# The attention output product by seven block products per pair of tiles, with its operands built beside late input tiles

## The chip, the core and the metric

One core of a Trainium2 chip runs the kernel as one program. The metric is the device time in microseconds, as the median over several executions. TensorE (PE in the profile) does the matmuls; VectorE (DVE), ScalarE (ACT) and GpSimd (POOL) prepare operands and take results out of PSUM; DMA queues, nearly all issued by SyncE (SP), move the data.

## The reference

One layer of a streaming encoder for a prompt of 1024 frames and a sample of 32 frames, model width 1024, all in float32. What matters here is the first part of the layer:

```python
h = rms_norm(x, g_mix)
z = h @ w_in
q, k, v, ch, cb, cc, ga, gb = jnp.split(z, SPLITS, axis=-1)
...
a = attn_core(q, k, v) @ w_attn_out
...
bo = (cb * conv) @ w_conv_out
x = x + (jax.nn.sigmoid(ga) * a + jax.nn.sigmoid(gb) * bo) @ w_mix_out
```

Behind it come a cross attention into 256 memory tokens, a squared-ReLU MLP of width 4096 and a final norm.

## The kernel before

All 1056 frames are kept transposed (features on the partitions) and cut into three chunks, CH, of 384, 384 and 288 columns: chunks 0, 1 and 2. A weight tile is 128 outputs by 1024 inputs (0.5 MB). Each float32 operand is split into a high and a low part (`split`: ScalarE casts the high part, line 120; VectorE subtracts, line 121), and a product takes three matmuls per 128 inputs: high by high, high by low, low by high (`gemm`, lines 176 to 178). A tile by one chunk is thus 24 matmuls.

The program writes a list of items (`item`, `run`) with the weights that each needs. `next_w` keeps two weights split ahead and one more in flight (`wr`); a STOP in the list of weights ends this running ahead, and `resume` takes it up again. The frame's scheduler then orders the instructions of each engine; each engine and SP's DMA queue works strictly in its order.

In the input projection the tiles from the second `b` on go in pairs (`x_pair`): two output tiles by chunks 0 and 1 form a two by two block product, and it is done by seven products of half the inputs (12 matmuls of 384 columns) instead of eight. For this the four operand kinds T2, N1, N3 and N4 are built once from the inputs (`x_kind`: line 801 to 805 differences, line 812 the high casts, lines 814 on VectorE and 816 on GpSimd the low parts, into tiles `tk` and the slots `X1`), and for each pair the weight sums s31 and s24 by four GpSimd additions (lines 834 to 837, `pair_issue`). `product` issues the matmuls (lines 852 to 854). Chunk 2 of each pair is done by plain products beside (`x_c2`, tiles `pa`). `x_start` opens the pairs with the products that need raw weights only; `x_steps` hangs weight splits and fetches on points of the pair before.

The last three pairs (LATE = 3) leave chunk 2 out. Their six tiles' chunk-2 products come as single items behind all pairs, with the raw weights loaded and split a second time; beside them the attention outputs, which were stored to `ao_d`, are loaded back into `ct` and split into the `Y` slots (`load_split`, line 1001), four per tile. Then `do_attn_out` multiplies them by `w_attn_out`: for tiles f = 0 to 3 all chunks, then f = 4 to 7 chunk by chunk (weights split again each time), each result times the gate `sg` into `m1_d`. Beside the later of these products the operands of the next stage (conv output, `bcp` from `bc_d`) are loaded and split.

GpSimd also prepares sums of `w_down` for the MLP in 32 pieces (`sum_load`, `sum_add`, `sum_step`, lines 726, 733, 734), spread over attention, pairs and late tiles.

In the trace, names such as `wh`, `wl` (weight high and low), `wr`, `wr2` (raw weights of a pair), `lt` and `ct` (temporaries), `acc` and `pa` (PSUM) are the tags of these tiles.

## Time and profile before

| | us |
|---|---|
| timed runs | 1795.58, 1793.97, 1791.87 |
| median | 1793.97 |
| profiled execution, its time | 1797.28 |
| its span | 1795.5 |
| attention, with parts of the projection | to about 414 |
| operand kinds and start of the pairs | about 414 to 458 |
| pairs | about 458 to 687 |
| late chunk-2 tiles | about 687 to 706 |
| attention output product | about 706 to 788 |
| conv output and mix | about 788 to 873 |

The lower rows are stretches of the profiled execution's time axis, told by the lines of TensorE's matmuls. A group's "idle before" is the time in which its engine stood still ahead of it, with what ended it; idle time of an engine matters where TensorE waits for that engine. In tables of windows the granted clock is that of TensorE, 1.00 being full speed.

### The profile page before, as it was taken

The page shows a single profiled execution, that of the slowest core. Times are in us where ns is not written, and L with a number is a line of the kernel's source. Part 1 is how long each engine was busy: PE and PEld are TensorE (multiplying, and loading weights), DVE is VectorE, ACT ScalarE, POOL GpSimd, SP SyncE. Part 2 cuts the span into 40 slices and gives each one's busy share as a digit, 9 for nine tenths or more (in the row PEclk, how much of TensorE's full clock was granted, in tenths as well). Part 3 has the DMA queues.
Part 4 walks back from the last instruction along what each step waited for, and adds up shares of the span by engine and source line. Part 5 has one row for each costly group of instructions (what it writes and reads, how often), then busy time and mean ns, then how long its engine had stood idle before and what let it go on. Part 6 is the DMA issues. An engine that isn't in the chain of part 4 may idle for free.

```text
span 1795.5 us, 30126 instructions
## 1 busy us (share of the span) xinstructions
PE 1750.8 (98%) x11030; PEld 1723.8 (96%) x11030; DVE 1190.2 (66%) x2081; ACT 816.0 (45%) x1573; POOL 738.6 (41%) x777
## 2 busy tenths in 40 slices
...
GB/s 180 144 66 141 104 151 99 148 90 152 120 99 90 167 97 265 219 246 317 252 227 208 246 213 240 248 168 151 142 122 137 162 304 207 163 134 200 195 248 102
DMA packets 177828, 312.50 MB, mean 174 GB/s; under 512 B 18032, under 2 KB 137616, under 8 KB 177552
## 3 DMA queue, kind: packets, MB, share of 16 engines
...
q14 instruction: 61, 0.50, 0.1%
...
## 4 chain that ended last, share of the span: by engine, by line
PE 80%; DMA 7%; DVE 5%; ACT 3%; issue 2%; POOL 2%; SPq 1%; POOLq 0%; DVEq 0%; ACTq 0%
PE acc L176 10%; PE acc L177 10%; PE acc L178 10%; PE acc L852 6%; PE acc L854 6%; PE acc L853 6%; PE acc L1648 5%; PE acc L1649 5%; PE acc L1647 5%; PE pa L177 2%; PE pa L176 2%; PE pa L178 2%; DVE wl L121 2%; PE pt L577 2%; DMA ct<-in_x 1%
## 5 line engine op out<-in xcount | busy, mean ns | idle before, releaser
L120 ACT CAST wh<-wr 128x1024 fp32r<-128x1024 f32 (+1 forms) x223 | 233.2, 1046 | 320.7 <-PE acc L1648 81.0
L121 DVE TENSOR_TENSOR wl<-wr,wh 128x1024 fp32r<-128x1024 f32 (+1 forms) x223 | 307.6, 1379 | 103.1 <-ACT wh L120 102.4
L253 POOL TENSOR_TENSOR xacc<-xacc,ct 128x384 f32<-128x384 f32 (+1 forms) x62 | 77.8, 1257 | 321.9 <-ACT ct L251 319.3
L176 PE MATMUL acc<-X,wh 128*128 128x384 f32 (+1 forms) x624 | 204.7, 328 | 1.1 <-ACT wh L120 1.1
L176 PE MATMUL acc<-Y,wh 128*128 128x384 f32 (+1 forms) x624 | 203.1, 326 | 2.3 <-DVE ct L1140 1.2
L177 PE MATMUL acc<-Y,wh 128*128 128x384 f32 (+1 forms) x624 | 203.0, 326 | 0.9 <-DVE Y L121 0.8
L177 PE MATMUL acc<-X,wh 128*128 128x384 f32 (+1 forms) x624 | 202.3, 324 | 1.0 <-DVE X L257 1.0
L178 PE MATMUL acc<-Y,wl 128*128 128x384 f32 (+1 forms) x624 | 202.8, 325 | 0.4 <-DVE wl L121 0.4
L178 PE MATMUL acc<-X,wl 128*128 128x384 f32 (+1 forms) x624 | 203.0, 325 | 0.0
L569 POOL TENSOR_SCALAR S<-S,rec 128x256 f32<-128x256 f32 (+1 forms) x132 | 124.1, 953 | 49.5 <-DVE rec L567 49.1
L176 PEld LDWEIGHTS acc<-Y,wh 128*128 128x128 f32 x624 | 117.8, 189 | 3.3 <-ACT Y L120 1.7
L177 PEld LDWEIGHTS acc<-X,wh 128*128 128x128 f32 x624 | 118.0, 189 | 2.7 <-DVE X L257 1.8
L176 PEld LDWEIGHTS acc<-X,wh 128*128 128x128 f32 x624 | 117.9, 189 | 2.6 <-ACT wh L120 1.3
L177 PEld LDWEIGHTS acc<-Y,wh 128*128 128x128 f32 x624 | 118.0, 189 | 1.8 <-DVE Y L121 1.8
L178 PEld LDWEIGHTS acc<-Y,wl 128*128 128x128 f32 x624 | 118.1, 189 | 0.8 <-DVE wl L121 0.8
L178 PEld LDWEIGHTS acc<-X,wl 128*128 128x128 f32 x624 | 117.9, 189 | 1.0 <-DVE wl L121 0.2
L1647 PE MATMUL acc<-Y,wh 128*128 128x384 f32 (+1 forms) x352 | 113.7, 323 | 0.7 <-DVE lt L1403 0.7
L1648 PE MATMUL acc<-Y,wh 128*128 128x384 f32 (+1 forms) x352 | 113.9, 324 | 0.1
L1649 PE MATMUL acc<-Y,wl 128*128 128x384 f32 (+1 forms) x352 | 113.6, 323 | 0.0
L120 ACT CAST wh<-s 128x1024 fp32r<-128x1024 f32 x50 | 52.2, 1050 | 90.6 <-PE acc L853 53.8
L121 DVE TENSOR_TENSOR Y<-ct,Y 128x384 fp32r<-128x384 f32 (+1 forms) x128 | 70.7, 582 | 29.5 <-ACT Y L120 29.5
L120 ACT CAST Y<-ct 128x384 fp32r<-128x384 f32 (+1 forms) x128 | 59.5, 486 | 60.2 <-DMA ct<-bc_d 14.6
...
## 6 DMA issues: line engine op xcount, KB each, us to landing
wr<-in_w_in SPq DMA_DIRECT2D x55, 512.0 KB, 3.3
wr<-in_w_up SPq DMA_DIRECT2D x48, 512.0 KB, 4.0
wr<-in_w_down SPq DMA_DIRECT2D x32, 512.0 KB, 3.8
wr<-wsum_d SPq DMA_DIRECT2D x32, 512.0 KB, 3.6
wl<-wl_d SPq DMA_DIRECT2D x28, 512.0 KB, 4.6
wr<-in_w_conv_out SPq DMA_DIRECT2D x24, 512.0 KB, 4.6
wr<-in_w_mix SPq DMA_DIRECT2D x24, 512.0 KB, 4.4
xacc<-in_w_down POOLq DMA_DIRECT2D x20, 512.0 KB, 3.7
```

Of the source, the lines that this page charges most:

```text
L120: act.copy(hi, src)
L121: dve.tensor_sub(lo, src, hi.bitcast(F32))
L176: pe.matmul(out, wh[:, a], hi, start=(k == 0), stop=False)
L177: pe.matmul(out, wh[:, a], lo, start=False, stop=False)
L178: pe.matmul(out, wl[:, a], hi, start=False, stop=(k == len(acts) - 1))
L569: pool_e.tensor_scalar_mul(stl[:, h, :nk], stl[:, h, :nk], rec[:, h : h + 1])
L852: pe.matmul(acc, wh[:, a], hi, start=(start and k == 0), stop=False, skip_group_check=True)
L853: pe.matmul(acc, wh[:, a], lo, start=False, stop=False, skip_group_check=True)
L854: pe.matmul(acc, wl[:, a], hi, start=False, stop=(k == 3), skip_group_check=True)
L1647: pe.matmul(a, wh[:, s], hi, start=(start and k == 0), stop=False, skip_group_check=True)
L1648: pe.matmul(a, wh[:, s], lo, start=False, stop=False, skip_group_check=True)
L1649: pe.matmul(a, wl[:, s], hi, start=False, stop=(stop and k == len(acts) - 1), skip_group_check=True)
```

## The change

Chunks 0 and 1 of the attention output product become four more pairs (`("o", f)` in XP, indices from NX = the old count on), of seven block products each; chunk 2 stays plain, eight products with their own split of the weights. The operand kinds for these pairs come from `ao_d` (`a_kind`, which also splits the plain operands that the pairs use, into the `X` slots instead of a pool of their own). They are built beside the late chunk-2 tiles, which are four pairs' now (LATE = 4, eight tiles). For these eight tiles the low weights are stored once when the pair splits them (`again`, `kept`, `wl_d`), and read back, so that VectorE does not subtract again. `a_start` opens the new pairs as `x_start` does the old ones. The pieces of the weight sums move: two more in the attention stage, one in nearly every pair, none beside the late tiles. The operands of the mix chunk that were split beside the attention product come later (`loads(1)` in `do_mix`).

```diff
-        for k in ((5, 8, 11, 14), (2, 5, 8, 11, 14), (2, 5, 8, 11, 14), (2, 5))[kv]:
+        for k in ((5, 8, 11, 14), (2, 5, 8, 11, 14), (2, 5, 8, 11, 14), (2, 5, 8, 11))[kv]:
...
         split(hi, lo, raws[key][src])
         wset[key, which] = (hi, lo)
+        at = again.get((key, which))
+        if at:
+            kept[at] = dram.tile([P, 1024], F32, name=nm("wl_d"))
+            sp.dma_start(kept[at], lo.bitcast(F32))
...
-    LATE = 3
+    LATE = 4
+    NX = len(XP)
+    XP += [(("o", f), ("o", f + 1)) for f in (0, 2, 4, 6)]
...
+    again.update({(("x", i), half + 1): tile_key(XP[i][half]) for i in range(NX - LATE, NX) for half in range(2)})
...
+        elif i in (NX - 1, len(XP) - 1):
+            todo = {w: resume for w in ("W1", "W4", "W3")}
...
-            if what == "W3" and (i % 3 or i == len(XP) - 1):
+            if what == "W3" and 0 < i != NX and i != NX + 1:
                 sum_load(True)
+            if i >= NX and what in ("B11", "W1"):
+                loads(1)
...
+    def a_kind(k):
+
+        b12, b22, b11, b21 = lt(), lt(), tmp(384), tmp(384)
+        for t, c, f in ((b12, 1, k), (b22, 1, k + 4), (b11, 0, k), (b21, 0, k + 4)):
+            sp.dma_start(t, ao_d[c][:, f])
+        ...
+        keep(0, k, b11)
+        keep(0, k + 4, b21)
+        keep(1, k + 4, b22)
+        n3, n1, t2, n4 = b22, b12, b11, b21
+        dve.tensor_sub(n3, b12, b22)
+        dve.tensor_sub(n1, b11, b12)
+        dve.tensor_sub(t2, b11, n3)
+        pool_e.tensor_tensor(n4, b21, t2, op=ALU.subtract)
+        for kind, x in (("T2", t2), ("N1", n1), ("N3", n3), ("N4", n4)):
+            ...
+            act.copy(hi, x)
+            if kind in ("T2", "N1"):
+                dve.tensor_sub(lo, x, hi.bitcast(F32))
+            else:
+                pool_e.tensor_tensor(lo, x, hi.bitcast(F32), op=ALU.subtract)
...
+    def a_start():
+        x_issue(NX, 4)
+        A = x_p1(NX)
+        A2 = x_p1(NX + 1)
+        x_p2(NX, A)
+        x_issue(NX, 3)
+        x_p2(NX + 1, A2)
+
+    steps = [lambda k=k: a_kind(k) for k in range(4)]
+    steps.append(lambda: [x_fetch(NX), x_issue(NX, 1), x_fetch(NX + 1)])
+    steps.append(lambda: [x_issue(NX, 2), x_issue(NX + 1, 1)])
+    last = [t for pair in XP[NX - LATE : NX] for t in pair]
+    steps[4:4] = [lambda: None] * (len(last) - 6)
+    for t, step in zip(last, steps):
+        item(do_in(t, [(2, step)], (2,)), tile_key(t))
+    worder.append(STOP)
+    item(lambda: todo.extend((aop, ao_d, 2, k) for k in range(NF)))
+    item(a_start)
+    for i in range(NX, len(XP)):
+        item(lambda i=i: x_pair(i, x_steps(i), {NX: 2, NX + 1: 1}.get(i, 0)))
     item(lambda: todo.extend((bcp, bc_d, 0, k) for k in range(NF)))
+    for f in range(NF):
+        item(do_attn_out(f, lambda f=f: [sum_done(), loads(1)]), ("w_attn_out", f))
...
@@ (do_mix)
+            if c == 0:
+                loads(1)
```

The order of the instructions moves at three places. In each row stand the line, the operation, output and inputs with their buffer numbers, the shape, and what the instruction waits for. Lines from 850 on are numbered four higher after the change, and higher still further down.

TensorE at the start of the first pairs, before: the end of N3's product for pair 0 (`tk_988` and `tk_989` with `wh_1015`), the T2 product of pair 1 (`wh_1026` and `wl_1027`, the split s24 of that pair), then N4's product (`X1_952`) and that of the plain chunk 1 (`X1_54`), both of pair 0:

```order
L852 MATMUL acc_1028_5668<-tk_988_5409,wh_1015_5565 128x384 [waits Activation_49]
L853 MATMUL acc_1028_5668<-tk_989_5410,wh_1015_5565 128x384 [waits Pool_49]
L854 MATMUL acc_1028_5668<-tk_988_5409,wl_1016_5566 128x384
L852 MATMUL acc_1044_5766<-tk_946_5282,wh_1026_5664 128x384 [waits Activation_49]
L853 MATMUL acc_1044_5766<-tk_947_5283,wh_1026_5664 128x384
L854 MATMUL acc_1044_5766<-tk_946_5282,wl_1027_5665 128x384 [waits DVE_49]
...
L852 MATMUL acc_1028_5668<-X1_952_5294,wh2_1002_5487 128x384 [waits DVE_49]
...
L852 MATMUL acc_1029_5669<-X1_54_356,wh_1008_5501 128x384 [waits DVE_49]
```

The same place after:

```order
L856 MATMUL acc_1030_5682<-tk_990_5423,wh_1017_5579 128x384 [waits Activation_49]
L857 MATMUL acc_1030_5682<-tk_991_5424,wh_1017_5579 128x384 [waits Pool_49]
L858 MATMUL acc_1030_5682<-tk_990_5423,wl_1018_5580 128x384
L856 MATMUL acc_1030_5682<-X1_954_5308,wh2_1004_5501 128x384 [waits DVE_49]
...
L857 MATMUL acc_1030_5682<-X1_993_5428,wh2_1004_5501 128x384 [waits Pool_49]
...
L856 MATMUL acc_1031_5683<-X1_54_356,wh_1010_5515 128x384 [waits DVE_49]
...
L856 MATMUL acc_1046_5780<-tk_948_5296,wh_1028_5678 128x384 [waits Activation_49]
L857 MATMUL acc_1046_5780<-tk_949_5297,wh_1028_5678 128x384
L858 MATMUL acc_1046_5780<-tk_948_5296,wl_1029_5679 128x384 [waits DVE_49]
```

The two products of pair 0 with `X1_954` and `X1_54`, 24 matmuls, now stand ahead of the T2 product of pair 1 (`wh_1028`, `wl_1029`) instead of behind it.

GpSimd at the same place, before: the last N4 low (`X1_991`), the sums s31 and s24 of pair 1, and the last N3 low (`tk_989`):

```order
L816 TENSOR_TENSOR tk_977_5380<-xk_969_5358,tk_976_5379 128x384 [waits Activation_49]
L816 TENSOR_TENSOR X1_991_5414<-xk_983_5390,X1_990_5413 128x384 [waits PE_49,Activation_49]
L834 TENSOR_TENSOR s31_1024_5658<-wr2_999_5455 128x512 [waits DMAHW7_49,DVE_49]
L837 TENSOR_TENSOR s31_1024_5658<-wr_998_5454,wr2_999_5455 128x512
L816 TENSOR_TENSOR tk_989_5410<-xk_981_5388,tk_988_5409 128x384 [waits DMAHW1_49,Activation_49]
L835 TENSOR_TENSOR s24_1025_5659<-wr_998_5454,s31_1024_5658 128x512 [waits Pool_49]
L836 TENSOR_TENSOR s24_1025_5659<-wr_998_5454,s24_1025_5659 128x512 [waits Pool_49]
```

And after:

```order
L816 TENSOR_TENSOR tk_991_5424<-xk_983_5402,tk_990_5423 128x384 [waits DMAHW1_49,DVE_49,Activation_49]
L834 TENSOR_TENSOR s31_1026_5672<-wr2_1001_5469 128x512 [waits DMAHW7_49,DVE_49]
L837 TENSOR_TENSOR s31_1026_5672<-wr_1000_5468,wr2_1001_5469 128x512
L816 TENSOR_TENSOR X1_993_5428<-xk_985_5404,X1_992_5427 128x384 [waits PE_49,Activation_49]
L835 TENSOR_TENSOR s24_1027_5673<-wr_1000_5468,s31_1026_5672 128x512 [waits Pool_49]
L836 TENSOR_TENSOR s24_1027_5673<-wr_1000_5468,s24_1027_5673 128x512 [waits Pool_49]
```

The last N4 low (`X1_993`) has moved behind the two s31 additions, and the last N3 low (`tk_991`) ahead of them; s24 stands last in both.

VectorE beside the late chunk-2 tiles, before: gate emits (`Gb2`), splits of attention outputs (`Y1`) and weight lows (`wl`):

```order
L662 TENSOR_TENSOR Gb2_1430_8247<-acc_1429_8222,R_141_767 128x288 [waits PE_49]
L121 TENSOR_TENSOR Y1_1400_8129<-ct_1398_8126,Y1_1399_8128 128x384 [waits DMAHW6_49,Activation_49]
L121 TENSOR_TENSOR wl_1446_8284<-wr_1444_8281,wh_1445_8283 128x1024 [waits DMAHW7_49,DVE_49,Activation_49]
L662 TENSOR_TENSOR Gb2_1448_8312<-acc_1447_8287,R_141_767 128x288 [waits PE_49]
L121 TENSOR_TENSOR Y1_1403_8135<-ct_1401_8132,Y1_1402_8134 128x384 [waits DMAHW0_49,Activation_49]
L121 TENSOR_TENSOR Y1_1406_8141<-ct_1404_8138,Y1_1405_8140 128x384 [waits DMAHW1_49,Activation_49]
L121 TENSOR_TENSOR Y1_1415_8188<-ct_1413_8185,Y1_1414_8187 128x384 [waits DMAHW2_49,Activation_49]
L121 TENSOR_TENSOR wl_1464_8349<-wr_1462_8346,wh_1463_8348 128x1024 [waits DMAHW3_49,DVE_49,Activation_49]
L121 TENSOR_TENSOR Y1_1418_8194<-ct_1416_8191,Y1_1417_8193 128x384 [waits DMAHW4_49,Activation_49]
```

After, the third kind of the four (`lt_1414`, `lt_1415`, `ct_1416`) with its differences (lines 1041 to 1043), its T2 and N1 lows (line 1053), and the weight lows of the first two new pairs (`wl_1478`, `wl_1482`):

```order
L121 TENSOR_TENSOR X1_1423_8142<-lt_1415_8126,X1_1422_8141 128x384 [waits DMAHW5_49,Activation_49]
L662 TENSOR_TENSOR Gb2_1466_8332<-acc_1465_8307,R_141_767 128x288 [waits PE_49]
L1041 TENSOR_TENSOR lt_1415_8126<-lt_1414_8125,lt_1415_8126 128x384 [waits DMAHW1_49,DVE_49,Pool_49]
L1042 TENSOR_TENSOR lt_1414_8125<-ct_1416_8127,lt_1414_8125 128x384 [waits DVE_49]
L1043 TENSOR_TENSOR ct_1416_8127<-ct_1416_8127,lt_1415_8126 128x384 [waits DVE_49]
L121 TENSOR_TENSOR wl_1478_8380<-wr_1471_8343,wh_1477_8379 128x1024 [waits DMAHW7_49,DMAHW2_49,Activation_49]
L662 TENSOR_TENSOR Gb2_1474_8372<-acc_1473_8347,R_141_767 128x288 [waits PE_49]
L1053 TENSOR_TENSOR tk_1425_8150<-ct_1416_8127,tk_1424_8149 128x384 [waits Activation_49]
L121 TENSOR_TENSOR wl_1482_8390<-s24_1480_8384,wh_1481_8389 128x1024 [waits DMAHW6_49,Activation_49]
L1053 TENSOR_TENSOR tk_1427_8154<-lt_1414_8125,tk_1426_8153 128x384 [waits Activation_49]
```

The differences and the lows of the kinds stand between the emits where the `Y` splits stood.

GpSimd beside the late tiles, before, has only the sums of `w_down`:

```order
L726 DMA xacc_1461_8339<-in_w_down 128x1024 [waits DMASW2_49]
L733 TENSOR_TENSOR ws_1443_8274<-ws_1443_8274 128x256 [waits DMASW1_49]
L733 TENSOR_TENSOR ws_1443_8274<-ws_1443_8274 128x256 [waits Pool_49] x3
L734 DMA wsum_d_97<-ws_1443_8274 128x1024 [waits Pool_49]
L726 DMA ws_1467_8380<-in_w_down 128x1024 [waits DMASW4_49]
```

After, it has the ends of the kinds (n4 on line 1044, lows of N4 and N3 on line 1055) and the weight sums of the second new pair (`s31_1491`, `s24_1492`):

```order
L1055 TENSOR_TENSOR tk_1429_8158<-lt_1415_8126,tk_1428_8157 128x384 [waits Activation_49]
L1044 TENSOR_TENSOR ct_1440_8202<-ct_1440_8202,ct_1439_8201 128x384 [waits DMAHW3_49,DVE_49]
L834 TENSOR_TENSOR s31_1491_8462<-wr2_1472_8344 128x512 [waits DMAHW7_49,DVE_49]
L837 TENSOR_TENSOR s31_1491_8462<-wr_1471_8343,wr2_1472_8344 128x512 [waits DMAHW7_49]
L1055 TENSOR_TENSOR X1_1454_8236<-ct_1440_8202,X1_1453_8235 128x384 [waits PE_49,Activation_49]
L1055 TENSOR_TENSOR tk_1452_8232<-lt_1438_8200,tk_1451_8231 128x384 [waits Activation_49]
L835 TENSOR_TENSOR s24_1492_8463<-wr_1471_8343,s31_1491_8462 128x512 [waits Pool_49]
L836 TENSOR_TENSOR s24_1492_8463<-wr_1471_8343,s24_1492_8463 128x512 [waits Pool_49]
```

The second new pair's s24 is behind the last kind's lows.

TensorE behind the late tiles, before, goes over to the attention output product with the `Y` operands:

```order
L177 MATMUL acc_1447_8287<-X2_105_573,wh_1409_8153 128x288
L178 MATMUL acc_1447_8287<-X2_104_572,wl_1410_8154 128x288
L176 MATMUL acc_1465_8352<-Y0_1360_7992,wh_1427_8218 128x384 [waits DVE_49,Activation_49]
L177 MATMUL acc_1465_8352<-Y0_1361_7993,wh_1427_8218 128x384
L178 MATMUL acc_1465_8352<-Y0_1360_7992,wl_1428_8219 128x384 [waits DVE_49]
```

After: raw-weight products (`X0` operands), T2, N3 and N4 of the first new pair, and then the T2 product of the second (`wh_1493`, `wl_1494`, the split of `s24_1492`):

```order
L858 MATMUL acc_1483_8393<-X0_1372_7985,wl_1470_8340 128x384 [waits DVE_49]
...
L856 MATMUL acc_1498_8478<-tk_1378_8001,wh_1481_8389 128x384 [waits DVE_49,Activation_49]
L857 MATMUL acc_1498_8478<-tk_1379_8002,wh_1481_8389 128x384
L856 MATMUL acc_1483_8393<-X0_1374_7989,wh_1469_8339 128x384 [waits Activation_49]
...
L856 MATMUL acc_1498_8478<-tk_1382_8009,wh_1488_8438 128x384 [waits DVE_49]
L857 MATMUL acc_1498_8478<-tk_1383_8010,wh_1488_8438 128x384 [waits Pool_49]
...
L856 MATMUL acc_1498_8478<-X1_1384_8013,wh2_1475_8375 128x384 [waits DVE_49]
...
L856 MATMUL acc_1520_8585<-tk_1378_8001,wh_1493_8468 128x384 [waits Activation_49]
L858 MATMUL acc_1520_8585<-tk_1378_8001,wl_1494_8469 128x384 [waits DVE_49]
```

The first product that needs s24 of the second new pair is now that last group, 108 matmuls behind the last late tile.

98 lines of the change are left out of this document (43 added, 55 removed).

## The prediction

> **What bounds the kernel now.** First the head of the page and its shares of the chain:
>
> ```profile
> span 1795.5 us, 30126 instructions
> PE 1750.8 (98%) x11030; PEld 1723.8 (96%) x11030; DVE 1190.2 (66%) x2081; ACT 816.0 (45%) x1573; POOL 738.6 (41%) x777
> PE 80%; DMA 7%; DVE 5%; ACT 3%; issue 2%; POOL 2%; SPq 1%; POOLq 0%; DVEq 0%; ACTq 0%
> ```
>
> TensorE is busy for 98% of the span, so a matmul taken out is worth its step unless something makes TensorE wait instead. The step is read from the timeline of TensorE:
>
> ```profile
> 669.94 0.33 PE L854 MATMUL acc<-X,wl 128*128 128x384 f32 x1
> ...
> 675.31 0.33 PE L852 MATMUL acc<-X,wh 128*128 128x384 f32 x1
> 443.21 0.29 PE L178 MATMUL pa<-X,wl 128*128 128x288 f32 x1
> ...
> 444.00 0.29 PE L178 MATMUL pa<-X,wl 128*128 128x288 f32 x1
> ```
>
> From 669.94 to 675.31 lie 31 steps: 0.1732 us per matmul of 384 columns. From 443.21 to 444.00 lie six: 0.132 us for 288 columns. A product of 24 matmuls of 288 columns thus takes 3.17 us.
>
> Next the windows around the stages that the change touches. The columns are window and length, busy time and count of PE, PEld, DVE, ACT and POOL, granted clock, DMA share, GB/s:
>
> ```profile
> 450.00:460.00 10.00, 7.25 (x32) 6.61 (x31) 4.56 (x5) 2.52 (x3) 5.88 (x6) 0.83 0.26 87
> 455.00:690.00 235.00, 234.11 (x1439) 233.79 (x1439) 169.45 (x207) 77.34 (x102) 144.90 (x139) 0.99 0.35 118
> 690.00:705.00 15.00, 15.00 (x115) 15.00 (x115) 13.90 (x19) 9.46 (x19) 6.00 (x8) 1.00 0.88 293
> 705.00:710.00 5.00, 5.00 (x32) 5.00 (x32) 4.52 (x7) 3.05 (x6) 4.36 (x5) 1.00 1.02 388
> 710.00:725.00 15.00, 12.96 (x54) 11.35 (x53) 8.97 (x16) 5.68 (x13) 4.81 (x7) 0.77 0.86 296
> 780.00:785.00 5.00, 5.00 (x40) 5.00 (x39) 3.29 (x5) 2.29 (x4) 0.00 (x0) 1.00 0.96 299
> ```
>
> The pairs (455 to 690) lose almost nothing. Two places do: 450 to 460 and 710 to 725. What TensorE waits for there:
>
> ```profile
> 450.99 0.34 PE L854 MATMUL acc<-tk,wl 128*128 128x384 f32 x1
> 453.44 0.45 PE L852 MATMUL acc<-tk,wh 128*128 128x384 f32 x1 [2.11 <-ACT wh L120]
> 454.70 0.69 PE L854 MATMUL acc<-tk,wl 128*128 128x384 f32 x1 [0.64 <-DVE wl L121]
> 457.74 0.45 PE L854 MATMUL acc<-tk,wl 128*128 128x384 f32 x1
> 715.70 0.40 PE L176 MATMUL acc<-Y,wh 128*128 128x288 f32 x1 [0.86 <-ACT Y L120]
> 718.14 0.61 PE L177 MATMUL acc<-Y,wh 128*128 128x288 f32 x1 [0.77 <-DVE Y L121]
> 719.44 0.45 PE L178 MATMUL acc<-Y,wl 128*128 128x288 f32 x1
> ```
>
> At 453.44 it is the first product of the second pair (T2, with the weight sum s24 of that pair) that has come up before its weights are split. At 715.70 the attention outputs read back (ct from ao_d) land too late for their splits Y, while the DMA engines are full. After each stop the matmuls go on at a longer step for some us (granted clock 0.83 and 0.77 in the two windows).
>
> **The change, part by part.** The sum is made against the profiled execution's own 1797.3 us; the median of the runs is 1794.0, that is 3.3 lower, and I take 3.3 off at the end.
>
> *Fewer matmuls.* Chunks 0 and 1 took 16 products of 24; now four pairs of seven block products of 12. 384 − 336 = 48 matmuls, 48 × 0.1732 = **−8.3 us**. The chunk-2 products (eight of 24 for the output, eight of the four a-pairs' tiles) are the same number as before.
>
> *The old entrance goes.* In 710 to 725 stand 54 matmuls. Nine of them (715.70 to 719.44) have 288 columns: 45 × 0.1732 + 9 × 0.132 = 9.0 us of work in 15. So 6.0 us were lost to the Y splits, and those splits no longer stand there: **−6.0 us**. What is late in their place comes below.
>
> The two starts below are costed from rows of the first start, where VectorE and GpSimd build the same four operands (T2, N1, N3, N4) and the weight sums s31 and s24 (min, median and max in ns behind an xN:; a timeline row has its start and length):
>
> ```profile
> L801 DVE TENSOR_TENSOR xk<-xk,xk x4: 548/559/1000, 418.9 to 436.9; 128x384 f32<-128x384 f32 x4
> L814 DVE TENSOR_TENSOR tk<-xk,tk x8: 551/1368/1642, 423.4 to 446.0; 128x384 fp32r<-128x384 f32 x8
> L816 POOL TENSOR_TENSOR tk<-xk,tk x4: 1001/1324/1957, 424.3 to 448.7; 128x384 fp32r<-128x384 f32 x4
> L834 POOL TENSOR_TENSOR s<-wr x3: 1276/1598/1605, 425.6 to 456.3; 128x512 f32<-128x512 f32 x3
> L121 DVE TENSOR_TENSOR wl<-s,wh x4: 1208/1212/1226, 440.7 to 455.0; 128x1024 fp32r<-128x1024 f32 x4
> L733 POOL TENSOR_TENSOR ws<-ws x4: 752/941/1605, 694.1 to 697.6; 128x256 f32<-128x256 f32 x4
> L120 ACT CAST wh<-wr 128x1024 fp32r<-128x1024 f32 (+1 forms) x223 | 233.2, 1046 | 320.7 <-PE acc L1648 81.0
> 447.98 0.44 DVE L662 TENSOR_TENSOR ct<-pa,R 128x288 f32<-128x288 f32 x1
> 423.29 1.08 POOL L816 TENSOR_TENSOR X<-xk,X 128x384 fp32r<-128x384 f32 x1 [14.93 <-ACT X L812]
> 434.03 1.59 POOL L836 TENSOR_TENSOR s<-wr,s 128x512 f32<-128x512 f32 x1
> 443.87 1.75 POOL L816 TENSOR_TENSOR X<-xk,X 128x384 fp32r<-128x384 f32 x1 [1.04 <-ACT X L812]
> 447.14 1.61 POOL L837 TENSOR_TENSOR s<-wr,wr 128x512 f32<-128x512 f32 x1
> L1001 SPq DMA_DIRECT2D ct<-ao_d x24: 319/336/437, 620.1 to 718.1; - x24
> DMA to landing us min/median/max: 1.6/2.8/6.4
> ```
>
> *The first start.* The order on TensorE moves there (shown above): the four products that need no weights of the second pair's s24 stand ahead of its T2 now, so 24 matmuls, 24 × 0.1732 = 4.2 us of work, fill the wait of 2.11 + 0.64. Of 450 to 460, 32 × 0.1732 = 5.5 us were work, so 4.5 were lost. What has to hold: GpSimd's last N4 split, which moved behind two weight sums. It stood at 443.87 before; the two sums end at 447.14 + 1.61 = 448.7, and its own 1.00 to 1.75 makes 450.5; TensorE comes to it ten matmuls after 451.2, at 452.9. I take **−4.0 us**; bounds 0 (another wait of that length stands there) and −4.5.
>
> *The new start of four pairs.* This is the cost. In the rows above VectorE and GpSimd take the short values alone and the long ones side by side.
>
> When is it needed? The late tiles began at 705.9 − 6 × 3.17 = 686.9 (the Y products start at 705.9). Pair 9's two chunk-2 tiles leave the pairs, 6.3 us, so the pairs end at 680.5. From there TensorE has 8 × 3.17 = 25.3 us of late tiles, 48 matmuls of raw-weight products (8.3) and 60 of the first pair (10.4), and then wants the T2 product of the second pair, with its s24: at 680.5 + 44.0 = **724.5**.
>
> When is it there? The order has one late tile ahead of the last pair's N4 product, so the lt tiles come free, and their loads go out, at about 683.5; with the median landing of 2.8 us (the ao_d rows) the first kind starts at 687. VectorE then has 24 instructions of 384 columns, six emits of 288 (0.44) and three weight lows up to the last kind's t2: at a mean of 1.0 (between the 0.56 of L801 and the 1.37 of L814), 24 × 1.0 + 6 × 0.44 + 3 × 1.21 = 30.3, so 717.3. Behind it on GpSimd: n4 of the last kind 1.3, two weight sums 3.2, the two lows 2.6, the two s24 halves 3.2 = 10.3, so 727.6; the cast wh 1.05 and the low 1.21 make 729.9. TensorE waits 5.4 us, and the slow step after it (as at 454.70 to 457.74, where 3 us went by at about half pace) costs some 2 more. I take **+8.0 us**, with the earlier products of this start (T2 to N4 of the first pair wait on the same lows, each by less) counted in it. Bounds: with nothing stretched VectorE needs 24 × 0.56 + 2.6 + 3.6 = 19.6 and GpSimd's tail is 9 us, so T2 is ready near 718, ahead of its time: 0. With no overlap at all, GpSimd's twelve 384-column operations of 1.0, seven weight sums of 1.28 and four reductions of 0.94 (24.7) come on top: 687 + 44.3 + 2.3 = 733.6, 9.1 late, 12 with a slow step of 3. The row nearest to this case is the first start itself, where L814's median of 1.37 says that most instructions were stretched, but not all: hence a value past the middle.
>
> The rule that would make it worse is in the Trainium skill, "SBUF — State Buffer", section "SBUF: two separate sides": a VectorE operation with two SBUF inputs and a GpSimd operation that reads SBUF exclude each other, and the later one is held for the whole instruction of the other. L814's longest 1.64 agrees (0.55 of its own and one of GpSimd's of 1.0). By the rule alone the term would be the serial bound, +12, not +8; it is the second rival.
>
> *Low weights read back.* Eight stores and eight loads of 0.5 MB, and late tiles without VectorE's lows (six of 1.21 before, 7.3 us less on VectorE where it is fullest: 13.90 of 15 from 690). The price is DMA. In SP's order stand, from the first low read back to the last ao_d load, eight lows, six raw tiles and two of the pairs' weights at 0.52 MB and ten ao_d loads at 0.20: 10.4 MB, with a reduction's load and store 11.4. They have from about 672 (the middle of the last pair) to 706: 335 GB/s, where the windows show 388 for 5 us and 293 for 15. A weight goes out two tiles ahead, 6.3 us, and such a load landed as follows in a later stage:
>
> ```profile
> wl<-wl_d SPq DMA_DIRECT2D x28, 512.0 KB, 4.6
> ```
>
> **+1.0 us**, since 335 lies midway between the two windows; bounds 0 (4.6 is below 6.3) and +5 (11.4 MB at 293 take 39 us, not 34).
>
> *The chunk-2 products at the end.* Eight products of 3.17 us in a row, each with a 0.5 MB weight, a bcp load and store: 0.9 MB per tile, near 300 GB/s, as 780 to 785 has (299, TensorE full). **+1.0**; bounds 0 and +5.
>
> *Edits with no price.* Eight more splits of w_attn_out (1.05 and 1.21 each) lie beside products of 3.17 us; the seven block products of a pair last 14.6 us for VectorE's about 11, as in the pairs of 455 to 690. Sums moved into every pair: GpSimd is busy 144.90 of 235 there; five more sums are some 15 us of it.
>
> Sum: −8.3 − 6.0 − 4.0 + 8.0 + 1.0 + 1.0 = −8.3, so 1789.0 on the profile's scale and **1785.7** as a median.
>
> **Rivals.** A change of under 0.2% (3.6 us) can't be told from none in this kernel.
>
> 1. *Second wait at the first start.* The reorder doesn't pay, since the wait moves to another weight sum. Speaks for it: GpSimd goes from sum to sum from 445.57 to 452. Against: 4.2 us of work now stand ahead. Gain 0 instead of 4: 1789.7.
> 2. *VectorE and GpSimd exclude each other through the whole new start* (the serial bound): +12 instead of +8, 1789.7. For: the 1.64 maximum. Against: GpSimd's eight operations from 423.29 to 435.62 take 4 × 1.0 + 4 × 1.28 = 9.1 alone and, with VectorE's two-input ones beside them in series (six of 0.56, one of 1.21), 13.7; they took 12.3, which is 0.7 of the way, as +8 is of +12.
> 3. *The new start is hidden.* VectorE, without the late tiles' weight lows, runs nearer 0.56: term 0 to 2, 1778 to 1780.
> 4. *Slower: the read-backs are late.* One mechanism at one place: the late tiles, where the low weight of each tile waits in SP's queue behind loads of ao_d, which wait for tiles that VectorE and GpSimd free. The weight then comes late, TensorE stops and goes on at the slow step, for each of eight tiles. Without the term for DMA the time is 1784.7; slower begins at 1797.6, so it decides from 13 us, 1.6 per tile. For: SP's order has those loads between the weights. Against: 6.3 us of lead. At 2.5 per tile, 20 us: 1804.7.
> 5. *No change*: rivals 1 and 2 together, 1793.7.
>
> **How the numbers follow.** Forecast 0.50; rival 1 alone 0.12; rival 2 alone 0.11; rival 3 0.10; rival 4 0.05; no change 0.12. Forecast, first three rivals: faster, 0.83; same 0.12; slower 0.05. The time is the forecast's, 1785.7. Range 1776 (rival 3 with both DMA terms at zero) to 1795 (no change's upper side, which leaves out rival 4 and little else).
>
> **What would show it.** Each step in the profile after: TensorE's count less by 48; no Y waits at the entrance; between 450 and 460 a window with clock near 1; one wait of some 5 us at the second new pair's first product, released by wh or wl; L1041 to L1055 on VectorE and GpSimd with medians near 1.0 and 1.3; late tiles at 3.17 us each and wl landing under 6 us. Wrong it would be most if the late tiles are spaced at more than 3.4 us, or if the first start shows a wait of 4 us at another product.

## The result and the profile after

The changed kernel takes **1820.13 us** (median of four, 1818.15 to 1823.2) beside 1794.42 for the kernel before: a ratio of **1.0144 [1.0126, 1.0162]**. It is 25.7 us slower where 8.3 less was forecast. The profiled execution took 1818.15 us (before: 1797.28), so the two traces that are compared here differ by 20.9 us; the other 4.8 lie between these executions and their medians, and no trace tells of them.

The head of the page after:

```profile
span 1816.4 us, 30154 instructions
PE 1749.4 (96%) x10982; PEld 1716.8 (95%) x10982; DVE 1234.2 (68%) x2119; ACT 829.1 (46%) x1599; POOL 780.6 (43%) x805
```

TensorE has the 48 matmuls less (11030 to 10982) and yet is busy for about as long, in a span longer by 20.9 us: matmuls run at a longer step, or wait. To see where, I use one count in all that follows, *lost time*: for every matmul the distance to the next one, less its own step (0.1732 us for 384 columns, 0.132 for 288, as the prediction read them), added up by stage. It takes in the wait and the slow step behind it, and is good to about 1 us in a stage (a missing record, a cut between stages a matmul off, a step 0.001 off). In the attention and in the rest, where matmuls of other shapes stand too, only the change tells something.

| lost, us | before | after | change | forecast |
|---|---|---|---|---|
| attention (before any edit, nearly) | 32.9 | 34.6 | +1.7 | 0 |
| first start | 10.3 | 10.3 | 0.0 | −4.0 |
| pairs | 2.4 | 8.3 | +5.9 | 0 |
| late tiles | 0.1 | 2.8 | +2.7 | +1.0 |
| entrance of the attention output product | 6.9 | gone | −6.9 | −6.0 |
| new start | none | 7.2 | +7.2 | +8.0 |
| new pairs | none | 4.1 | +4.1 | 0 |
| chunk-2 products in a row | none | 5.6 | +5.6 | +1.0 |
| conv output, first 40 us of mix | 2.4 | 4.5 | +2.1 | 0 |
| the rest | 50.6 | 56.9 | +6.3 | 0 |

The sum is 28.7; with 48 × 0.1732 = 8.3 taken off it is 20.4, which accounts for the 20.9. In other words: the six terms of the forecast (five stages and the matmuls) came to +0.3, where −8.3 was forecast, and the stages without a term brought +20.1.

One part of the lost time is not a matter of the kernel's order. Behind some stops the granted clock falls to 0.50 for 3.4 or 6.8 us, and the matmuls of 384 columns stand 0.32 us apart; behind other stops of the same kind it stays at 1.00. The attention shows it: at 74.8 in before and at 75.1 in after TensorE waits 0.99 us, for the same instruction, and from 75.0 to 78.4 the granted clock is 1.00 in before and 0.50 in after. This one stretch is the +1.7 of the attention. About half the length of such a stretch is lost. In after the chunk-2 row holds 3.4 us of it and the first start 6.8; in before the first start holds 6.8 and the entrance 6.8; the other stages up to the mix hold none in either trace.

Windows of after that answer to those of before (same columns):

```profile
430.00:460.00 30.00, 24.62 (x127) 22.65 (x126) 26.30 (x30) 14.88 (x28) 21.27 (x15) 0.89 0.40 129
440.00:450.00 10.00, 7.26 (x38) 6.38 (x37) 9.47 (x13) 6.87 (x13) 4.76 (x5) 0.85 0.45 138
450.00:460.00 10.00, 9.14 (x40) 8.51 (x40) 7.00 (x10) 3.80 (x6) 6.51 (x5) 0.81 0.21 67
455.00:690.00 235.00, 227.80 (x1388) 225.29 (x1387) 175.97 (x207) 78.86 (x107) 156.33 (x154) 1.00 0.46 157
525.00:535.00 10.00, 8.06 (x53) 7.83 (x52) 9.54 (x12) 3.03 (x4) 9.24 (x12) 1.00 0.16 61
690.00:705.00 15.00, 15.00 (x110) 15.00 (x109) 9.17 (x16) 9.55 (x16) 3.00 (x3) 1.00 0.97 346
720.00:730.00 10.00, 7.73 (x43) 7.41 (x43) 9.90 (x12) 5.64 (x11) 7.73 (x7) 1.00 0.28 102
740.00:760.00 20.00, 19.30 (x111) 18.98 (x111) 18.29 (x22) 9.86 (x13) 10.49 (x6) 1.00 0.46 148
800.00:810.00 10.00, 7.92 (x52) 7.44 (x53) 5.50 (x10) 4.24 (x6) 0.00 (x0) 0.94 0.79 238
820.00:840.00 20.00, 18.60 (x105) 17.69 (x104) 13.37 (x18) 9.22 (x15) 5.48 (x4) 1.00 0.90 308
```

and four of before: the first start, the same stretch of the pairs, a part of the attention output product, and the conv output product. (Before's attention output product ends at about 805, and not at 788 as the table of stages ahead of the prediction has it: behind its chunk-2 products, which end at 788.0, stand four products of chunk 1, and conv output's 192 matmuls of chunk 0 follow.)

```profile
430.00:460.00 30.00, 24.14 (x127) 22.62 (x126) 23.25 (x28) 13.35 (x25) 20.90 (x16) 0.89 0.34 114
520.00:530.00 10.00, 10.00 (x65) 10.00 (x64) 9.11 (x12) 1.67 (x2) 8.73 (x12) 1.00 0.31 103
760.00:780.00 20.00, 20.00 (x125) 20.00 (x124) 10.85 (x16) 7.23 (x10) 0.00 (x0) 1.00 0.59 199
805.00:839.00 34.00, 33.56 (x192) 33.24 (x191) 23.13 (x35) 16.35 (x27) 6.26 (x6) 1.00 0.95 329
```

The first start has 127 matmuls in 30 us before and after: nothing was gained. The pairs stop at 525 to 535, where before has no stop (its 520 to 530). What TensorE waits for, from the timeline (start, length, instruction, and in brackets the idle time and what ended it):

```profile
444.60 0.45 PE L856 MATMUL acc<-tk,wh 128*128 128x384 f32 x1 [0.93 <-ACT wh L120]
447.66 0.69 PE L858 MATMUL acc<-tk,wl 128*128 128x384 f32 x1 [1.49 <-DVE wl L121]
457.46 0.44 PE L856 MATMUL acc<-X,wh 128*128 128x384 f32 x1 [0.65 <-DVE lt L937]
533.63 0.44 PE L856 MATMUL acc<-X,wh 128*128 128x384 f32 x1 [1.94 <-DVE lt L937]
710.41 0.40 PE L178 MATMUL acc<-X,wl 128*128 128x288 f32 x1 [1.10 <-DMA wl<-wl_d]
721.59 0.45 PE L858 MATMUL acc<-X,wl 128*128 128x384 f32 x1 [2.31 <-DVE wl L121]
730.19 0.41 PE L856 MATMUL acc<-tk,wh 128*128 128x384 f32 x1 [0.87 <-ACT tk L1051]
735.75 0.44 PE L856 MATMUL acc<-tk,wh 128*128 128x384 f32 x1 [1.30 <-DVE lt L931]
743.12 0.33 PE L856 MATMUL acc<-tk,wh 128*128 128x384 f32 x1
807.71 0.40 PE L176 MATMUL acc<-X,wh 128*128 128x288 f32 x1 [1.28 <-ACT wh L120]
893.11 0.44 PE L178 MATMUL acc<-X,wl 128*128 128x384 f32 x1 [0.78 <-DMA wl<-wl_d]
898.61 0.83 PE L207 MATMUL pq<-ones,xacc 128*128 128x1 f32 x6 [0.70 <-POOL xacc L253]
```

The row of 743.12 is the first product of the second new pair, which waits for nothing. No wait in this list is longer than 2.31 us. The loss is many short stops, some of them with slow steps behind them.

### The profile page after: what moved, and what is told of

The parts are those of the page before. It is cut to its first block, busy times and chain, and to the rows that moved or that the text cites. A ratio compares the mean times of both kernels' runs of the same rounds, so it can differ in the third digit from the quotient of the medians.

```text
span 1816.4 us, 30154 instructions
## 1 busy us (share of the span) xinstructions
PE 1749.4 (96%) x10982; PEld 1716.8 (95%) x10982; DVE 1234.2 (68%) x2119; ACT 829.1 (46%) x1599; POOL 780.6 (43%) x805
## 4 chain that ended last, share of the span: by engine, by line
PE 39%; DMA 8%; DVE 5%; issue 3%; POOL 2%; ACT 2%; SPq 1%; POOLq 0%; DVEq 0%; ACTq 0%
PE acc L1696 5%; PE acc L1695 5%; PE acc L1697 5%; PE acc L856 3%; PE acc L858 3%; PE acc L857 3%; PE acc L176 3%; PE acc L177 3%; PE acc L178 3%; DVE wl L121 2%; DMA wr<-in_w_mix 1%; PE pa L177 1%; PE pa L176 1%; PE pa L178 1%; ACT wh L120 1%
## 5 line engine op out<-in xcount | busy, mean ns | idle before, releaser
L176 PE MATMUL acc<-X,wh 128*128 128x384 f32 (+1 forms) x1136 | 368.3, 325 | 6.5 <-ACT wh L120 3.5
L178 PE MATMUL acc<-X,wl 128*128 128x384 f32 (+1 forms) x1136 | 367.2, 324 | 3.8 <-DVE wl L121 1.9
L177 PE MATMUL acc<-X,wh 128*128 128x384 f32 (+1 forms) x1136 | 365.6, 322 | 1.2 <-DVE X L257 1.2
L176 PEld LDWEIGHTS acc<-X,wh 128*128 128x128 f32 x1136 | 214.7, 189 | 9.6 <-ACT wh L120 4.6
L178 PEld LDWEIGHTS acc<-X,wl 128*128 128x128 f32 x1136 | 214.7, 189 | 6.8 <-DVE wl L121 3.3
L177 PEld LDWEIGHTS acc<-X,wh 128*128 128x128 f32 x1136 | 214.9, 189 | 2.9 <-DVE X L257 1.9
L856 PE MATMUL acc<-X,wh 128*128 128x384 f32 x464 | 156.4, 337 | 6.2 <-DVE lt L937 3.7
L858 PE MATMUL acc<-X,wl 128*128 128x384 f32 x464 | 154.2, 336 | 4.1 <-DVE wl L121 4.1
L857 PE MATMUL acc<-X,wh 128*128 128x384 f32 x464 | 155.4, 335 | 0.0
L1695 PE MATMUL acc<-X,wh 128*128 128x384 f32 (+1 forms) x352 | 113.5, 323 | 0.3 <-ACT X L120 0.3
L1696 PE MATMUL acc<-X,wh 128*128 128x384 f32 (+1 forms) x352 | 113.3, 322 | 0.2 <-DVE X L121 0.2
L1697 PE MATMUL acc<-X,wl 128*128 128x384 f32 (+1 forms) x352 | 113.1, 321 | 0.0
L120 ACT CAST wh<-s 128x1024 fp32r<-128x1024 f32 x58 | 60.6, 1050 | 113.3 <-PE acc L857 66.8
L178 PE MATMUL pa<-X,wl 128*128 128x288 f32 x336 | 99.3, 296 | 0.7 <-DVE wl L121 0.7
L177 PE MATMUL pa<-X,wh 128*128 128x288 f32 x336 | 99.7, 297 | 0.0
L176 PE MATMUL pa<-X,wh 128*128 128x288 f32 x336 | 99.2, 295 | 0.0
L856 PEld LDWEIGHTS acc<-X,wh 128*128 128x128 f32 x464 | 87.1, 188 | 8.8 <-DVE lt L937 4.8
L733 POOL TENSOR_TENSOR xacc<-xacc 128x256 f32<-128x256 f32 x92 | 83.6, 909 | 21.2 <-DMA xacc<-in_w_down 17.9
```

The costliest lines, as they stand in the source:

```text
L120: act.copy(hi, src)
L176: pe.matmul(out, wh[:, a], hi, start=(k == 0), stop=False)
L177: pe.matmul(out, wh[:, a], lo, start=False, stop=False)
L178: pe.matmul(out, wl[:, a], hi, start=False, stop=(k == len(acts) - 1))
L856: pe.matmul(acc, wh[:, a], hi, start=(start and k == 0), stop=False, skip_group_check=True)
L857: pe.matmul(acc, wh[:, a], lo, start=False, stop=False, skip_group_check=True)
```

## The experiments

Every time stands beside runs of the kernel before on the same chip. "Lost" is the count of the table, and it comes from one profiled execution each. In e3, e5, e10, e11 and e12 that execution took 2.6 to 5.9 us more than the kernel's median. And the stretches at half clock come and go: after, e4, e5 and e9 have the same instructions in the old pairs, and lose 8.4, 10.8, 8.4 and 10.5 us there; in e4 and e9 one stretch of 3.4 us (from 535.5 and 534.6) stands behind the stop that after has at 533.63, in the other two none. A difference of 2 or 3 us in one stage can thus be half clock alone, and it is named below where it is in the numbers.

### The sums of w_down

At 533.63 TensorE waits for VectorE's L937. The queues of VectorE and of GpSimd there, in after:

```profile
525.47 4.30 DVE L644 SCALAR_TENSOR_TENSOR ct<-u,prm,ct 128x290 f32<-128x290 f32 x4
530.56 2.55 DVE L644 SCALAR_TENSOR_TENSOR ct<-u,prm,ct 128x384 f32<-128x384 f32 x2 [0.32 <-ACT ct L642]
533.03 0.55 DVE L937 TENSOR_TENSOR lt<-acc,s 128x384 f32<-128x384 f32 x1
527.39 0.95 POOL L733 TENSOR_TENSOR xacc<-xacc 128x256 f32<-128x256 f32 x1
529.84 0.73 POOL L733 TENSOR_TENSOR xacc<-xacc 128x256 f32<-128x256 f32 x1
531.97 0.72 POOL L733 TENSOR_TENSOR xacc<-xacc 128x256 f32<-128x256 f32 x1
```

The conv's taps (L644 on VectorE, L646 on GpSimd) share this stretch with a sum of w_down (L733), which before had no piece in this pair. L937, 0.55 us of work, is behind the taps in VectorE's queue. Two kernels tell whether the sums are the cause: after with the old places of the sums, and before with the new ones.

```diff
 e1: after, sums of attention and pairs as before, five left for the chunk-2 products
-        for k in (... (2, 5, 8, 11))[kv]:
+        for k in (... (2, 5))[kv]:
-            if what == "W3" and 0 < i != NX and i != NX + 1:
+            if what == "W3" and (i % 3 if i < NX - 1 else i not in (NX, NX + 1)):
-        item(do_attn_out(f, lambda f=f: [sum_done(), loads(1)]), ...
+        item(do_attn_out(f, lambda f=f: [sum_done(), sum_load(True) if f < 5 else None, loads(1)]), ...
 e2: before, with after's sums
-        for k in (... (2, 5))[kv]:
+        for k in (... (2, 5, 8, 11))[kv]:
-            if what == "W3" and (i % 3 or i == len(XP) - 1):
+            if what == "W3" and i:
```

> The changed kernel with the w_down sums of the attention stage and of the first thirteen pairs placed as before (two fewer in attention, none in pairs 3, 6 and 9); the five pieces left go beside chunk-2 output products. Theory S (sums in every pair make VectorE and GpSimd late there, and the two in attention delay the first start): the loss in the pairs falls from about 8.4 to 2 to 4 us, the first start gains 2 to 3, the chunk-2 products lose 1 to 3 more, and the time falls from 1820 to about 1812. Theory R (the stores of the low weights and the transfers are what disturbs the pairs): the pairs lose 7 to 8 as they do now, and the time stays within 3 us of 1820.

Measured 1825.07, 1.0162 [1.014, 1.0184]. The pairs lose 2.9 instead of 8.3, and the stretch of 525 to 535 is whole again:

```profile
523.00:533.00 10.00, 10.00 (x65) 10.00 (x64) 7.38 (x9) 1.72 (x3) 6.47 (x9) 1.00 0.48 142
```

But the five pieces, 0.5 MB each to load and as much to store, now lie where DMA is full, and the conv output product and the mix behind it lose 16.4 instead of 4.5. The time got no better. (6.8 us of that stage of e1 are at half clock, so some 3.4 of the loss.)

> The kernel before with the sums placed as in the changed one: two more in attention, one in every pair from the second on, two beside late tiles. Theory S: the pairs lose 4 to 6 us more than before, the late stage gains about 2 (fewer transfers at the entrance of the output product), so 1796 to 1799. Theory R: no stall in the pairs appears; 1791 to 1794.

Measured 1796.4, 1.0006 [0.9994, 1.0017]. The pairs lose 6.4 instead of 2.4, with the same stop in before's kernel:

```profile
520.00:530.00 10.00, 8.71 (x57) 8.48 (x55) 9.54 (x11) 3.60 (x8) 9.78 (x12) 1.00 0.21 72
```

Here the stages behind gave it back (the attention output product loses 4.1 instead of 6.9; its sums are gone there, and so is the stretch of 6.8 us at half clock that before has in it, so chance may have a part). So the sums cost the pairs 4.0 to 5.4 us: shown in both directions. Both kernels also settle the first start. TensorE's order there goes with the sums: e1 has the old one (48 matmuls on tk in a row) and loses 9.0, e2 the new one and loses 9.1. Both have 3.4 us at half clock in it where before and after have 6.8, which makes up the difference from their 10.3. The order itself is worth nothing.

### The read-backs

```diff
 e3: after, every late tile's low built by VectorE again
-    ... for i in range(NX - LATE, NX) for half in range(2)})
+    ... for i in () for half in range(2)})
```

> The changed kernel without the stores and the read-back of the low weights: the eight late tiles split their weights again on VectorE. Theory R: the pairs lose some 3 us less, the loads of the attention outputs land in about 3 instead of 5 us, so the kinds start earlier and the late tiles lose nothing; the time falls to 1812 to 1816. Rival theory V (VectorE is the bound of the new start): eight lows of 1.2 us on VectorE make the new start 3 to 8 us later; 1822 to 1828.

Measured 1818.75, 1.0129 [1.0109, 1.015]. The DMA saved brings nothing: in the trace the late tiles lose 4.5 (2.8 in after) and the new pairs 11.5 (4.1). That execution took 5.9 us more than e3's median, and it has 17 us at half clock in the new start, so how much VectorE's eight lows cost can't be told from it. The fourth rival, that the read-backs are what makes it slower, falls.

### The chunk-2 products in a row

ScalarE's casts of the weights and SP's loads for them in after, then what one load of this weight took from issue to landing in this stage of after (784 to 817) and of before (750 to 788):

```profile
797.72 1.05 ACT L120 CAST wh<-wr 128x1024 fp32r<-128x1024 f32 x1 [3.16 <-DMA wr<-in_w_attn_out]
806.61 1.04 ACT L120 CAST wh<-wr 128x1024 fp32r<-128x1024 f32 x1 [3.52 <-DMA wr<-in_w_attn_out]
793.81 0.44 SPq L138 DMA_DIRECT2D wr<-in_w_attn_out  x1
800.05 0.34 SPq L138 DMA_DIRECT2D wr<-in_w_attn_out  x1
wr<-in_w_attn_out SPq DMA_DIRECT2D x5, 512.0 KB, 6.0
wr<-in_w_attn_out SPq DMA_DIRECT2D x7, 512.0 KB, 3.4
```

The raw weights have two buffers. A buffer is free again when the weight is split, and its next load takes 6.0 us: about 8.5 us for a turn of two weights, so one in 4.2 us, where a product takes 3.17. A window at DMA's 0.79 is not at its limit; the ring of buffers is.

```diff
 e4: after, four raw buffers for these weights, fetched one earlier
+        if key[0] == "w_attn_out" and key[1] % 2:
+            raw = PW["pool"].tile([P, 1024], F32, tag="wr2", bufs=2, name=nm("wr2"))
+        else:
             raw = wp.tile([P, 1024], F32, tag="wr", bufs=2, name=nm("wr"))
...
+        if key[0] == "w_attn_out" and not fetched and ... worder[wpos[0]][0] in ("w_attn_out", "w_conv_out"):
+            fetch_w()
```

> The changed kernel with four raw-weight buffers instead of two for the chunk-2 output products (every other weight into a buffer of the pairs), each fetched one product earlier. Theory W (two raw buffers with landings of 6 us cannot feed products of 3.2 us): the chunk-2 stage's loss falls from 4.9 to 0 to 1.5 and that of the conv output by some 1 to 2; 1814 to 1817. Rival (the transfers themselves fill the DMA engines): the landings get longer and the stage loses 4 to 6 as now; 1818 to 1821.

Measured 1813.1, 1.009 [1.0069, 1.0112], 7.0 less than after. The row loses 0.7 instead of 5.6, and runs at a higher DMA share than in after:

```profile
800.00:810.00 10.00, 10.00 (x78) 10.00 (x77) 6.55 (x10) 4.63 (x7) 0.00 (x0) 1.00 0.92 313
```

So the ring was this stage's bound: shown. (The three loads of this weight that e4 issues from 784 on land in 4.2 us, so what the two more buffers did and what the shorter landing did is not told apart; some 1.7 of after's 5.6 is its stretch at half clock, from 808.8.) Spreading the row does it too:

```diff
 e5: after, chunk 2 of the last two new pairs inside them, four in a row behind
-        if i >= NX - LATE:
+        if NX - LATE <= i < NX + 2:
...
-    for f in range(NF):
-        item(do_attn_out(f, lambda f=f: [sum_done(), loads(1)]), ...
+    for f in range(4):
+        item(do_attn_out(f, lambda f=f: [sum_done(), loads(2)]), ...
```

> The changed kernel with the chunk-2 output products of the last two new pairs inside those pairs, with the pairs' own split weights, so that four weights fewer are loaded and split and only four chunk-2 products stand in a row. Theory W (weights come too slowly for eight products of 3.2 us in a row): the chunk-2 loss falls from 5.6 to about 2, conv output from 4.2 to about 3; and the last two pairs, 6 us longer each, lose 1 to 2 less: 1813 to 1816. Rival: the loads of the chunk-2 operands, twice as fast beside the pairs, make the pairs lose as much as is gained: 1818 to 1822.

Measured 1813.55, 1.0093 [1.0076, 1.0109]. The row loses 0.1, but the conv output product 7.0 (4.2 in after), some 1.7 of it by 3.4 us at half clock.

### What the conv output product pays

Two kernels ask this of before: one with only bcp's chunk-2 loads moved into the mix, and one with the old products in after's order, chunks 0 and 1 first, then eight chunk-2 products in a row.

```diff
 e6 and e10: before
-    item(lambda: todo.extend((bcp, bc_d, 2, k) for k in range(NF)))
-    todo.extend((bcp, bc_d, 1, k) for k in range(NF))
+    todo.extend((bcp, bc_d, c, k) for c in (1, 2) for k in range(NF))
...
+            if c == 0:
+                loads(1)
 e10 alone
-    for f in range(4):
-        item(do_attn_out(f, range(3), ...
+    for f in range(NF):
+        item(do_attn_out(f, (0, 1), ...
...
+    for f in range(NF):
+        item(do_attn_out(f, (2,), [(2, lambda: loads(1))]), ("w_attn_out", f))
```

> The kernel before with one part of the change alone: the mix stage's chunk-2 operands (bcp of chunk 2) are loaded and split one per chunk-0 mix product instead of beside the attention output products. Theory M (this move explains the 4 us that the changed kernel loses around the norm sums behind the chunk-0 mix products): about 3 to 5 us slower, 1797 to 1800, with the loss in the same place. Rival (the late stage is merely carried over from the conv stage's full DMA engines): no change, 1793 to 1796.

Measured 1794.52, 0.9996 [0.9986, 1.0007]: the place of these loads costs nothing.

> The kernel before with the output product in the changed one's order of chunks: chunks 0 and 1 of all eight tiles, then eight chunk-2 products in a row with one bcp load each; the mix operands load later, as in the changed kernel. Theory W: the eight in a row lose 4 to 6 us by their weights as in the changed kernel and conv output 2 to 4 more; 1800 to 1804. If the loss there comes from what the new pairs leave behind (stores, splits, sums), it is not seen here: 1794 to 1796.

Measured 1800.25, 1.0029 [1.0015, 1.0043]; before beside it 1795.16. In the trace chunks 0 and 1 lose 3.9 and the row of chunk-2 products 2.2, where before's whole product loses 6.9, and the conv output product loses 6.5 instead of 1.2, with no half clock in either. The window of that product in e10, beside that of before above:

```profile
806.00:840.00 34.00, 29.86 (x163) 27.66 (x162) 20.88 (x29) 13.21 (x22) 6.86 (x5) 1.00 0.86 289
```

163 matmuls in 34 us, where before does its 192. The order alone, without pairs, low read-backs or new sums, thus costs 5.1 us by the medians, and the trace has its loss behind the place where the order was changed. (Its execution took 1806.11, 5.9 above the median, so the 5.3 more of conv output are at the upper end.) Why the conv output product is the one to pay stays open. DMA is not busier ahead of it than in before: 0.45 from 770 to 780 and 0.70 from 780 to 806 in e10, 0.83 from 775 to 788 and 0.82 from 788 to 805 in before. The stops in it wait for the split of an operand (812.35, 1.06 us), for VectorE's work on a gate (823.12, 1.49) and for the low parts of weights.

### More pairs with late tiles, and all reliefs together

```diff
 e7: after
-    LATE = 4
+    LATE = 5
```

> The changed kernel with five pairs' chunk-2 tiles late instead of four: ten late tiles, 6.3 us more cover for the building of the new operands, at two more tiles' loads, stores and read-backs. If the new start is bounded by the chain from the last old pair through VectorE (the forecast's mechanism): its loss falls from about 7 to 2 or less, 1814 to 1816. If the DMA engines are what is short there: the late tiles lose 2 to 4 more and little is gained, 1818 to 1822.

Measured 1820.62, 1.0135 [1.0121, 1.0149]. The new pairs lose 0.6 and the row 1.6, but one stop in the old pairs and the read-backs take it all back, and the new start, with 6.3 us more cover, still loses about 6:

```profile
642.06 0.69 PE L856 MATMUL acc<-X,wh 128*128 128x384 f32 x1 [5.42 <-ACT s L907]
705.23 0.40 PE L178 MATMUL acc<-X,wl 128*128 128x288 f32 x1 [2.01 <-DMA wl<-wl_d]
```

e8 puts e5, more raw buffers for the row of four, and the sums of two old pairs into the last two new ones together; e12 adds six buffers lt (four in after) and moves a third sum.

```diff
 e8 (e12 in brackets), besides e5 and e4's buffers
-            if what == "W3" and 0 < i != NX and i != NX + 1:
+            if what == "W3" and i not in (0, 3, 9, NX, NX + 1):     (0, 3, 9, 12, NX)
 e12
-        ... tag="lt", bufs=PW.get("lt", 4) ...
+        ... tag="lt", bufs=PW.get("lt", 6) ...
```

> The changed kernel with three edits that the runs so far point to: chunk 2 of the last two new pairs inside them, every other weight of the four chunk-2 products left into a buffer of the pairs (four raw buffers, each fetched one product earlier), and the w_down sums of pairs 3 and 9 moved into the last two new pairs as second pieces. If the losses are separate, as theories S and W have it, they add: pairs 8.3 to about 4, chunk-2 and conv output 9.8 to about 3, so 1820 to 1807 to 1810. If the DMA engines' total is the bound, what is taken out at one place comes back at the next, and the time stays at the 1813 of the single edits. Either way above the kernel before, since the new start (7 us) and the new pairs (4) are untouched.

Measured 1808.35, 1.0067 [1.0053, 1.0081]: pairs 3.6, row 0.1, but new start 8.4 and conv output 7.8 (with 3.4 and 6.8 us at half clock).

> The kernel with the three edits together, with six lt buffers and with the sum of the last old pair moved to the second new pair, which takes its four additions out of GpSimd's queue between the kinds. Theory B: the new start's loss falls from 8.4 to about 3, so 1808 to 1802 to 1805. If the kinds' engine time is the bound: 1807 to 1810. The kernel before (1795) is beaten by neither, since conv output still loses 7 and the new pairs 5.

Measured 1805.71, 1.0053 [1.0038, 1.0069]. This is the best version of the change that I found, 14.4 us under after and still 10.9 over before. Its largest loss is the conv output product's 8.6, some 3.4 of it by 6.8 us at half clock. Its operand loads, moved from the first chunk of the mix to the second:

```diff
 e14: e12, and
-            if c == 0:
+            if c == 1:
```

> The kernel with the edits together and six lt buffers, and the eight chunk-1 operand loads of the conv output moved from its chunk-0 products to the chunk-0 mix products, those of chunk 2 to the chunk-1 conv products. If conv output loses by what it asks of the DMA engines (a weight, three or four operand tiles and every other a store in 4.2 us) on top of the queue it inherits: its loss falls from 8.6 to about 4 and the time from 1806 to 1801 to 1803. If only the inherited queue and the weights count: 7 to 9, and 1804 to 1807.

Measured 1808.52, 1.0071 [1.0054, 1.0088]: the conv output product loses 5.2 instead of 8.6 (half of this difference is half clock), and the mix behind it 5.3 instead of 0.3. The loss moves on with the loads. From the chunk-2 row to the mix, DMA runs at 0.81 to 0.95 of its time in e12 and e14, and here what one stage saves the next one pays.

### The new start

Its loss, 7.2, is near the forecast's 8.0, and the stretch from the first kind to the last one's t2 was 30.9 us (698.7 to 729.6) against 30.3. The instructions (min, median, max in ns):

```profile
L1041 DVE TENSOR_TENSOR lt<-lt,lt x4: 558/990/1544, 699.3 to 726.8; 128x384 f32<-128x384 f32 x4
L1053 DVE TENSOR_TENSOR tk<-lt,tk x4: 546/1068/1640, 702.7 to 732.1; 128x384 fp32r<-128x384 f32 x4
L1055 POOL TENSOR_TENSOR X<-ct,X x4: 996/1172/1326, 703.0 to 734.9; 128x384 fp32r<-128x384 f32 x4
lt<-ao_d SPq DMA_DIRECT2D x8, 192.0 KB, 5.1
```

Medians near 1.0 and 1.1, as forecast, and landings of 5.1 us where 2.8 was taken. Five kernels tried what binds here: VectorE's eight lows of T2 and N1 as copies on ScalarE (e9), six lt buffers (e11), both (e13), and pair 12's sum moved to pair 14, alone (e15) and with both (e16). In e9, e13 and e16 the low parts of T2 and N1 are left out: copies stand in their place.

```diff
 e9, e13, e16
-                dve.tensor_sub(lo, x, hi.bitcast(F32))
+                act.copy(lo, x)
 e11, e13, e16
-        ... tag="lt", bufs=PW.get("lt", 4) ...
+        ... tag="lt", bufs=PW.get("lt", 6) ...
 e15, e16
-            if what == "W3" and 0 < i != NX and i != NX + 1:
+            if what == "W3" and i not in (0, 12, NX):
```

> The changed kernel with VectorE's eight low parts of T2 and N1 in the new operand building replaced by copies on ScalarE, which leaves the low parts of these operands wrong; nothing else differs. If VectorE's chain is the bound of the new start (the forecast's mechanism: 24 instructions at about 1.0 us), taking 8 of them out shortens it by 6 to 8 us and the new start loses 1 to 2 instead of 7; 1813 to 1815. If the loads or GpSimd bound it, it stays near 7; 1818 to 1821.

> The changed kernel with six lt buffers instead of four. The new operands' kinds go through four lt tiles, two per kind, and the last kinds' loads were issued only at 710.5 to 713, when GpSimd's lows of the first kinds had let go of them; the run without VectorE's lows kept the loss of the new start, and its loads were later still. Theory B (buffers: two kinds in flight, each with a landing of 5 us and GpSimd's queue behind it): the third kind's loads go out some 8 us earlier, the last one's some 5, and the new start's loss falls from 7.2 to 2 to 4; 1814 to 1817. If VectorE's and GpSimd's time on the kinds is the bound, it stays at 6 to 8 and the time at 1818 to 1821.

> The changed kernel with six lt buffers and with VectorE's eight lows of T2 and N1 replaced by copies on ScalarE (the low parts of these operands are wrong). Each edit alone left the new start's loss (9.2 and 9.4 against 7.2): with VectorE relieved, the last kinds' loads were late; with the loads early, VectorE and GpSimd stretched each other. If these two bounds lie at about the same place, the two edits together bring it to 2 to 4. If a third thing binds (the weight sums behind the kinds on GpSimd, the weights' landings), it stays at 6 or more.

> The changed kernel with one w_down sum moved: that of the last old pair, whose four GpSimd additions stand between the new operands' kinds, goes to the second new pair. Theory P (VectorE and GpSimd take turns in the new start: from 713 to 740 their operations on SBUF add up to 29.7 us at the lengths they have alone, in 26.7 us, and the same holds in the three runs that kept the loss): three to four us of additions less on GpSimd shorten new start and new pairs together from 11.3 to 7 to 9; 1816 to 1818. If the order of VectorE's queue alone binds: 11 to 12 and 1819 to 1821.

> The changed kernel with three edits at the new start: six lt buffers, no VectorE lows of T2 and N1 (ScalarE copies, wrong low parts), and the last old pair's sum moved to the second new pair. Theory P: together 7 to 8 us of the two engines' work is out of the stretch, and new start and new pairs fall from 13.7 (with the first two edits) to 6 to 8; 1812 to 1815. If the order of the queues binds: 12 to 14, 1818 to 1820.

| | time | ratio | new start lost | new pairs lost | at half clock in the start | TensorE's waits in the start |
|---|---|---|---|---|---|---|
| after | 1820.13 | 1.0144 [1.0126, 1.0162] | 7.2 | 4.1 | 0 | 6.1 |
| e9 lows away | 1813.74 | 1.0096 [1.008, 1.0111] | 9.4 | 2.9 | 6.8 | 6.1 |
| e11 six lt | 1819.71 | 1.0134 [1.0119, 1.0148] | 9.2 | 3.0 | 3.4 | 6.3 |
| e13 both | 1819.4 | 1.0136 [1.0119, 1.0154] | 9.6 | 4.1 | 6.8 | 8.0 |
| e15 sum moved | 1823.17 | 1.0146 [1.0125, 1.0168] | 6.3 | 10.3 | 3.4 | 3.6 |
| e16 all three | 1818.69 | 1.013 [1.0103, 1.0158] | 8.8 | 3.8 | 3.4 | 5.0 |

The last column adds up the idle time of TensorE from the first product of the new start to the second new pair's T2. (e15's new pairs have another 6.8 us at half clock.)

By the count none shortened the start by more than 1 us; by the waits alone e15 took 2.5 off it in its trace and e16 1.1, and the others nothing. e9's gain of 6.4 lies elsewhere (the chunk-2 row loses 1.0 there). e15 moved the cost into a new pair, where one stop is 4.85 long. e9 has one of 4.15 in the start, for a cast of the last kind, and this cast had itself waited 5.80 us for VectorE's t2. e16's start still waits, and its GpSimd and VectorE wait themselves:

```profile
751.50 0.69 PE L858 MATMUL acc<-X,wl 128*128 128x384 f32 x1 [4.85 <-DVE wl L121]
737.85 0.69 PE L856 MATMUL acc<-tk,wh 128*128 128x384 f32 x1 [4.15 <-ACT tk L1051]
737.28 0.51 ACT L1051 CAST tk<-ct 128x384 fp32r<-128x384 f32 x1 [5.80 <-DVE ct L1043]
722.39 0.44 PE L858 MATMUL acc<-X,wl 128*128 128x384 f32 x1 [1.80 <-DVE wl L121]
713.63 1.27 POOL L835 TENSOR_TENSOR s<-wr,s 128x512 f32<-128x512 f32 x1 [3.81 <-DMA wr<-in_w_attn_out]
727.31 1.24 DVE L121 TENSOR_TENSOR X<-lt,X 128x384 fp32r<-128x384 f32 x1 [2.54 <-ACT X L120]
```

The first row is e15's, the next two e9's, the other three e16's. In e9 the last kind's t2 starts at 735.75, 6.7 us later than in after, though VectorE has eight instructions fewer: ahead of it VectorE stands for 3.45 us (to 730.76) until ScalarE has cast a weight sum. With VectorE's lows, the buffers and the sum out of the way (e16), GpSimd stands for 3.81 us until a weight lands, and VectorE for 2.54 until ScalarE has cast. e12, which has the six lt and the moved sum too, shows the same: e8's stops from 723.33 to 729.84 (6.5 us lost) are down to 0.8 there, and the first products of the start wait in their place, 2.74 us at 716.15 for a weight's low part. So **what binds the new start stays open**. Less work on VectorE does not shorten it (e9), nor do six lt buffers (e11); the sum has a part in it (e15), and the three together left 5.0 of 6.1 us of waits. The landing of the new pairs' first weights, in a stretch where DMA is at 0.94 (705 to 715 in after), and the order of the queues behind it are left; no run took that away.

## Why the prediction was wrong

**Right.** The 48 matmuls are gone, and with them 8.3 us. The old entrance is gone (−6.9 for −6.0). The new start costs 7.2 for 8.0, and VectorE's stretch has the length that was forecast (30.9 for 30.3).

**New start: the number right, the path wrong.** One wait of 5.4 us at the second new pair's T2 was forecast, with 2 us of slow steps behind it. That product (743.12) does not wait at all; the low part of its weight is done at 742.0. The losses stand ahead of it, at the first new pair's raw-weight products (721.59) and at its T2 and N3 (730.19 to 735.75), which the forecast had wait "each by less", and there is no half clock in them. Both ends of the sum also came later than forecast: the first kind at 699.3 for 687, the T2 at 743.1 for 724.5. And by the forecast's chain e9, with a quarter of these VectorE instructions fewer, should have hidden most of the term; TensorE's waits there are 6.1 us as in after. That 7.2 came out near 8.0 is luck.

**First start, −4.0 measured as 0.0.** The step that failed is "24 matmuls … fill the wait". They do: the T2 of pair 1, at 461.74 now, no longer waits. But pair 0's own T2, which stands ahead of them, does, for the split of its own s24 (444.60 and 447.66). ScalarE's casts of pair 0's sums, in before and in after:

```profile
438.40 1.99 ACT L120 CAST wh<-s 128x1024 fp32r<-128x1024 f32 x2
443.51 1.99 ACT L120 CAST wh<-s 128x1024 fp32r<-128x1024 f32 x2
```

They come 5.1 us later (GpSimd's last addition for them ends at 440.4 instead of 435.6), where TensorE began the stage only 1.8 later. e2 has the same stops with before's work (442.04 and 445.10), so they belong to the new order. This is the first rival, given 0.12. The check that was made looked at the one operand known to move (N4 on GpSimd), and not at VectorE, busy for 9.47 of 10 us from 440 to 450.

**"Edits with no price": sums moved into every pair, +4.0 to +5.4.** GpSimd's 144.90 of 235 was read as room. An average over 235 us says nothing of the 10 us beside the conv's taps, where before's window shows VectorE at 9.11 and GpSimd at 8.73 of 10. Forecast at nothing, it is the largest failed term for which runs show the cause in both directions (e1, e2).

**New pairs, 0 taken, 4.1 lost.** "VectorE's about 11 of 14.6" was carried over from the old pairs. In the new pairs VectorE also multiplies the results by the gates (L1059) and splits the chunk-2 attention outputs: it is busy for 18.29 of 20 in 740 to 760, and the longest stops behind it (748.48, 0.70 us, and 765.12, 1.07 us) are for weight lows of VectorE. That this load is the cause is argued from the window; no run took it away by itself.

**Chunk-2 row, +1.0 taken, 5.6 lost.** It was costed as a rate (0.9 MB per tile near 300 GB/s), where the ring of two raw buffers with 6.0 us of landing sets the pace (e4). The row that was read for it, before's at 780 to 785, was only four products long, and its weights had gone out from 760.91 to 773.44, beside products of 4.2 us and with a landing of 3.4: it showed no steady pace.

**Late tiles, +1.0 taken, 2.7 lost**, inside its bounds of 0 to 5: the longest stop is 1.10 at 710.41, a low weight behind ao_d loads in SP's order. The mechanism of rival 4 is there, at a fifth of what would have decided; without the read-backs the time is the same (e3).

**Downstream, nothing taken.** The prediction ended at the chunk-2 row. Behind it the conv output product lost 3.0 more in after (5.3 more in e10's trace, from the order alone). The rest, beyond 890, lost 6.3 more; of it 3.6 between 887 and 908, from the stops at 893.11 and 898.61 on. Between 1030 and 1480 after has 13.7 us at half clock where before has 6.8, worth some 3.4 us, which is enough for the 2.7 left. e10, with the chunk-2 order alone, has 1.7 of the 6.3; what causes the 3.6 was not tried, and stays open. The 1.7 in the attention is the stretch at half clock of 75.0 to 78.4, ahead of every edit.

None of the rivals described the whole: the slower side was one mechanism at one place, and it came from several small ones instead.
